# First chunk of a two-layer mixer kernel: eight one-block passes instead of five, with the rounding moved between engines

## The chip, the core and the metric

The kernel runs on one core of a Trainium2 chip. The metric is the device time of one execution in microseconds (us), the median of several runs. Times in the profile are us unless marked ns.

## What is computed

The program is a two-layer diffusion block over 1024 latent tokens and 256 context tokens, 1024 features wide. What matters here is the very beginning of layer 0, the modulated input and the first quarter of its input projection:

```
sh, sc, gt = split(silu(c) @ w_mod + b_mod, 3)     # c: a row of 1024, w_mod: 1024 x 3072
h  = x * (1 + sc) + sh                             # x: 1024 tokens x 1024
csh, csc, cgt = split(silu(c_ctx) @ w_mod + b_mod, 3)
hc = ctx * (1 + csc) + csh                         # ctx: 256 tokens x 1024
a, ga, u, v, gb = split([h; hc] @ w_in, ...)       # a: pooling branch, ga: its gate, ...
```

All else (pooling, spatial gating, Fourier mixing, latent attention, the output projections, the norms) comes after and is not touched.

## The kernel before

A float32 product is made of three passes of TensorE on rounded operands: an operand is split into a high part (rounded to the type fp32r) and a low part (the rest, rounded as well), and high x high, high x low and low x high are added up in PSUM. `split` (L103 to L107) makes both parts: a copy by VectorE (DVE) or ScalarE (ACT) gives the high part, a subtraction by GpSimd (POOL) or VectorE the low part.

The features lie on partitions, in eight row blocks of 128 (KT is 8, P is 128). The 1280 tokens (T) lie in the free dimension, in three segments, `SEG`: 512, 512 and 256 (context). The first chunk, 256 columns of the weight `ab_w_in` (called a1), is summed over the row blocks into five PSUM tiles `acc` (two column halves of each of the two long segments, and one tile for the short one), so that work can begin as soon as the first row block of `w_mod`, `w_in` and of the transposed input is there. `PASS` (L273) cuts the eight row blocks into passes of 1, 2, 2, 2 and 1. Per pass there are:

- `load` (L314): on the SyncE queue, the columns of `w_mod` for shift and scale of these row blocks (tiles `wm`), the rows of a1 (`raw_a`), and the rows of the transposed input (S, in the code `xT`).
- `mods` (L331): 16 float32 products of SiLU(c), SiLU(c_ctx) with `wm` (tile `md`), copied by DVE to `mrow` (L339). Each shows as two records in a trace.
- `mods_turn` (L341): transposes of `mrow` on TensorE (tile `pj`), then on DVE a sum (L347), two additions of the bias (L351) and 1 + scale (L352). The outcome is the tile `mod`: one column of shift and one of scale per row block.
- `split` of the a1 rows, and `fill` (L297) for each of five blocks of 256 tokens: one ACT operation per row block makes x * scale + shift in place (L303), then DVE makes the high part, and DVE (even blocks) or POOL (odd blocks) the low part; both cover two row blocks at once in a pass of two.
- `products` (L354) for each of the five `acc` tiles: three per row block (L363), twice that for the short segment.

`pin` keeps operations in the order of the program on their engine, so the loop sets what stands behind what: `mods` of the next pass stands on TensorE behind `acc` tile 0 of this one, and `mods_turn` behind tile 1 (tiles 2 and 3 in the first pass). Loads run one pass ahead: `load(p + 1)` is issued ahead of pass p. The tag wm has three buffers of 256 columns. Behind the last pass, `ga1`, the next 256 columns of `ab_w_in`, are split (ACT the high part, DVE the low one), and its products (`ps_mm`, L210) begin when the last `acc` product is through.

The whole of this takes the first 60 us of the program. The rest of the order is set by a planner, and by pattern strings for the attention.

Of the kernel before, what the change touches and what calls it, by code (L numbers as in the profile page):

```python
# [9 lines left out]
F32 = mybir.dt.float32  # L10
F32R = mybir.dt.float32r
AF = mybir.ActivationFunctionType
# [5 lines left out]
P = 128  # L18
# [3 lines left out]
T = S + C  # L22
NT = T // P
NL = S // P
KT = D // P
# [14 lines left out]
def _f(ap):  # L40
    return ap.bitcast(F32)


def hybrid_block(tc, A):
    nc = tc.nc
    ctx = ExitStack()
    with ctx:
        _body(nc, tc, A, ctx)


def _body(nc, tc, A, ctx):
    def pool(name, bufs=1, side=None, space=None, stack=ctx):
        kw = {}
        if side:
            kw["side"] = side
        if space is not None:
            kw["space"] = space
        return stack.enter_context(tc.tile_pool(name=name, bufs=bufs, reuse_waits="tile", **kw))
# [37 lines left out]
    def slot(pl, k, shape, dt, name):  # L96
        return pl.tile(shape, dt, tag=f"s{k}", name=name)


    def pin(ins):  # L100
        return tc.keep_in_program_order(ins)

    def split(dH, dL, src, h="v", l="p", ordered=False):  # L103

        keep = pin if ordered else (lambda ins: ins)
        keep(nc.vector.tensor_copy(dH, src) if h == "v" else nc.scalar.copy(dH, src))  # L106
        keep((nc.gpsimd if l == "p" else nc.vector).tensor_sub(dL, src, _f(dH)))  # L107
# [65 lines left out]
    def w_cols(w, c0, n):  # L173
        return w[:, c0:c0 + n].rearrange("(k p) n -> p k n", p=P)
# [65 lines left out]
    ld = pool("ld", stack=st0)  # L240
# [9 lines left out]
    mod0 = hp.tile([P, 16, 2], F32, name="mod0")  # L250
    mod1 = hp.tile([P, 16, 2], F32, name="mod1")
    S567 = [slot(keep if sl == 6 else var, sl, [P, 4096], F32, f"S{sl}") for sl in (5, 6, 7)]

    def ps_0(name, shape=(P, 512), tag="md"):
        return psums[-1].tile(list(shape), F32, tag=tag, name=name, bufs=1)
# [14 lines left out]


    SEG = ((0, 512), (512, 512), (1024, 256))
    PASS = ((0, 1), (1, 3), (3, 5), (5, 7), (7, 8))  # L273
    NP = len(PASS)
    st1 = ExitStack()
    w_a1 = w_cols(A["ab_w_in"], 256, 256)
    a1 = [wp.tile([P, 2048], F32R, tag=f"w{c_}", name=f"w{c_}_a1").rearrange("p (k n) -> p k n", k=KT) for c_ in "HL"]
# [3 lines left out]
    K0 = {k: (0, i) for i, k in enumerate((0, 1, 2, 7))} | {k: (1, k - 3) for k in range(3, 7)}  # L281
    K1 = {k: (k // 4, k % 4) for k in range(KT)}
    h0 = [[slot(keep if b in (0, 1) else var, b, [P, 2, 4, 512], F32R, f"h0_{b}") for b in (2 * sg, 2 * sg + 1)] for sg in range(2)]
    h0 += [slot(var, 4, [P, 2, KT, 256], F32R, "h0_4")]

    def tok(hs, at_, hl, k, a0, n):

        if a0 >= S:
            return hs[2][:, hl, k, a0 - S:a0 - S + n]
        half, i = at_[k]  # L290
        return hs[a0 // 512][half][:, hl, i, a0 % 512:a0 % 512 + n]


    at = ((0, 0), (0, 1), (0, 2), (1, 0), (1, 1), (2, 0), (2, 1), (1, 2))
    xT = [S567[i][:, j * T:(j + 1) * T] for i, j in at]

    def fill(p, b):  # L297

        k0, k1 = PASS[p]
        cnd = 0 if b < 4 else 1  # L300
        ts = slice(b * 256, (b + 1) * 256)
        for k in range(k0, k1):
            pin(nc.scalar.activation(xT[k][:, ts], xT[k][:, ts], AF.Identity,  # L303
                                     bias=mod0[:, k, cnd:cnd + 1], scale=mod0[:, 8 + k, cnd:cnd + 1]))
        i, j = at[k0]
        src = S567[i][:, j * T:(j + k1 - k0) * T].rearrange("p (k t) -> p k t", t=T)[:, :, ts]
        if b < 4:
            half, i = K0[k0]
            d = h0[b // 2][half][:, :, i:i + k1 - k0, b % 2 * 256:b % 2 * 256 + 256]
        else:  # L310
            d = h0[2][:, :, k0:k1, :]
        split(d[:, 0], d[:, 1], src, "v", "p" if b % 2 else "v", True)

    def load(p):  # L314
        k0, k1 = PASS[p]
        w = (k1 - k0) * P
        c = slice(k0 * P, k1 * P)
        wm = []
        for a in range(2):
            wm.append(ld.tile([P, KT, 256], F32, tag="wm", name=f"wm{p}{a}", bufs=3)[:, :, 0:w])  # L320
            src = w_cols(A["ab_w_mod"], a * D + k0 * P, w)
            n = KT if p else KT // 2
            for k in range(0, KT, n):
                nc.sync.dma_start(out=wm[a][:, k:k + n, :], in_=src[:, k:k + n, :])
        raw = wp.tile([P, 1024], F32, tag="raw", name=f"raw_a1_{p}", bufs=3)[:, 0:2 * w].rearrange("p (k n) -> p k n", n=256)
        nc.sync.dma_start(out=raw, in_=w_a1[:, k0:k1, :])
        for k in range(k0, k1):
            nc.sync.dma_start(out=xT[k], in_=A["xT"][k * P:(k + 1) * P, :])
        return wm, raw

    def mods(p, wm):  # L331
        md = ps_0(f"md{p}")
        w = (PASS[p][1] - PASS[p][0]) * P
        for a in range(2):
            for k in range(KT):
                g = k % 4
                pin(nc.tensor.matmul(md[32 * g:32 * g + 32, a * w:(a + 1) * w], lhsT=scp[:, k, :],
                                     rhs=wm[a][:, k, :], start=(k < 4), stop=(k >= 4)))
        pin(nc.vector.tensor_copy(mrow[:, :2 * w], md[:, :2 * w]))  # L339

    def mods_turn(p):  # L341
        pj = ps_0(f"pj{p}", (P, 4, 4, 32))
        k0, k1 = PASS[p]
        n = 2 * (k1 - k0)
        for j in range(n):
            pin(nc.tensor.transpose(pj[:, j].rearrange("p g c -> p (g c)"), mrow[:, j * P:(j + 1) * P], ident))
        pin(nc.vector.tensor_reduce(out=msum[:, :n], in_=pj[:, :n, :, 0:2].rearrange("p j g c -> p j c g"), axis=AX.X, op=ALU.add))  # L347
        m = mod0.rearrange("p (a k) c -> p a k c", a=2)[:, :, k0:k1, :]
        bm = cols[:, R_BM0:R_BM0 + 16].rearrange("p (a k) -> p a k", a=2)[:, :, k0:k1]
        for c2 in range(2):  # L350
            pin(nc.vector.tensor_add(m[:, :, :, c2], msum[:, :n, c2].rearrange("p (a k) -> p a k", a=2), bm))  # L351
        pin(nc.vector.tensor_scalar(m[:, 1], m[:, 1], 1.0, 1.0, op0=ALU.mult, op1=ALU.add))  # L352

    def products(p, u):  # L354
        sg, j_ = UNITS[u]
        a0, nt = SEG[sg]
        js = (0, 1) if j_ is None else (j_,)
        for j in js:
            c = slice(j * P, (j + 1) * P)
            o = acc[u][:, j * nt:(j + 1) * nt] if j_ is None else acc[u]  # L360
            for k in range(*PASS[p]):
                for n, (w, x) in enumerate(((0, 0), (0, 1), (1, 0))):
                    pin(nc.tensor.matmul(o, lhsT=a1[w][:, k, c], rhs=tok(h0, K0, x, k, a0, nt),  # L363
                                         start=(k + n == 0 and j == js[0]), stop=(k == KT - 1 and n == 2 and j == js[-1])))

    W.add("ga1", w_cols(A["ab_w_in"], 768, 256), KT, 256, eng=("s", "v"))
    raws = {}
    wm, raws[0] = load(0)
    mods(0, wm)
    mods_turn(0)  # L370
    for p in range(NP):
        if p < NP - 1:
            wm, raws[p + 1] = load(p + 1)
        k0, k1 = PASS[p]
        split(a1[0][:, k0:k1, :], a1[1][:, k0:k1, :], raws[p], "v", "p", True)
        if p == NP - 2:
            W.fetch("ga1", 1e9)
        for b in range(5):
            fill(p, b)
        if p == NP - 1:  # L380
            for i in range(2):
                W.step("ga1", i)
        for b in range(5):
            products(p, b)
            if p < NP - 1 and b == (0 if p else 2):
                mods(p + 1, wm)
            if p < NP - 1 and b == (1 if p else 3):
                mods_turn(p + 1)
    st0.close()

# [230 lines left out]
    for ch in (1, 0):  # L621
# [11 lines left out]
        if ch == 1:  # L633
            for u, (sg, j_) in enumerate(UNITS):
                o, n = OFF[sg], SEG[sg][1]
# [171 lines left out]
    for t in range(NT):  # L807
        src = A["x"][t * P:(t + 1) * P, :] if t < NL else A["ctx"][(t - NL) * P:(t - NL + 1) * P, :]
# [758 lines left out]
```

## Time and profile before

| | |
|---|---|
| median of 3 runs | 1137.46 us (1137.27 to 1138.54) |
| the profiled execution, its own time | 1138.53 us |
| its span, first to last instruction | 1136.7 us |
| PE busy | 1077.7 us, 95% of the span |
| PE weight loads busy | 917.5 us, 81% |
| DVE busy | 827.1 us, 73% |
| ACT busy | 456.3 us, 40% |
| POOL busy | 524.2 us, 46% |
| mean granted TensorE clock | 0.977 of full speed |
| last product of the first chunk issued, first of ga1 begins | 60.38 us |

PE is TensorE's matmuls, PEld its weight loads, SPq SyncE's DMA queue. Busy shares are means over stages that have different limits. Matmuls are pipelined: rows of PE overlap, and the distance from one start to the next says more than a duration. "[0.74 <-POOL h L107]" behind a row means that the engine was idle for 0.74 us and what ended that.

### The profile page before, as it was taken

What the parts mean: (1) busy time and instruction counts of PE and PEld (TensorE: products, weight loads), DVE (VectorE), ACT (ScalarE), POOL (GpSimd) and SP (SyncE); (2) the same over time, 40 slices, a digit from 0 to 9 for tenths busy, and PEclk for the clock granted to TensorE, in tenths of its full rate; (3) what the DMA queues carried; (4) which work ended last, traced back from release to release, by engine and by line L of the source; (5) the groups of instructions that cost most, each with busy time, mean ns of one, the idle gap of its engine ahead of it and who ended that gap; (6) DMA issues with size and microseconds to landing.
All of it is one profiled execution on the core that took longest, in us unless ns stands there. A gap on an engine that the chain in (4) does not pass through costs nothing.

```text
span 1136.7 us, 16517 instructions
## 1 busy us (share of the span) xinstructions
PE 1077.7 (95%) x5986; PEld 917.5 (81%) x5986; DVE 827.1 (73%) x1713; ACT 456.3 (40%) x1096; POOL 524.2 (46%) x449
## 2 busy tenths in 40 slices
PE   6999999899999999999999999999999999999884
PEld 4788887778878888897888877889899898887664
DVE  4683547899987767767200175988999989977998
ACT  3421222221211233531021244887888888860000
POOL 2362321555563433112481234855556556657442
PEclk7999999989999999999999999999999999999897
DMA  9630110235543322404311110000000010214221
GB/s 345 222 95 29 47 56 1 60 108 168 166 156 122 104 101 71 148 1 154 106 56 37 34 53 22 1 1 2 1 1 1 1 57 1 75 38 143 85 77 67
DMA packets 46993, 85.58 MB, mean 75 GB/s; under 512 B 2928, under 2 KB 27632, under 8 KB 46912
## 3 DMA queue, kind: packets, MB, share of 16 engines
q1 hardware_dynamic: 44096, 76.60, 21.2%
q0 software_dynamic: 1664, 5.84, 1.4%
q10 hardware_dynamic: 1152, 2.10, 0.5%
q8 instruction: 47, 0.77, 0.3%
q14 instruction: 34, 0.28, 0.1%
HBM read 76.13 MB, written 8.39 MB: 74 GB/s over the span
## 4 chain that ended last, share of the span: by engine, by line
PE 65%; DVE 23%; issue 4%; POOL 3%; ACT 3%; DMA 1%; SPq 0%; DVEq 0%; POOLq 0%; ACTq 0%
PE ps_mm L210 19%; PE ps_o L442 10%; PE s L1096 8%; PE ps_n L442 6%; PE av L1314 5%; PE pt_p L1289 5%; PE acc L363 2%; PE ps_y L1049 2%; DVE acc L499 2%; DVE mx L1255 2%; DVE rz L1477 2%; PE ps_c L210 2%; DVE rz L1446 1%; PE pq L1106 1%; DVE rs_tz L227 1%
## 5 line engine op out<-in xcount | busy, mean ns | idle before, releaser
L1096 PE MATMUL s<-kT,qT 96*128 96x512 f32 (+1 forms) x576 | 147.8, 370 | 3.7 <-ACT p L1267 2.7
L1267 ACT ACTIVATE p<-s,mx 128x512 f32<-128x512 f32 (+1 forms) x192 | 118.7, 624 | 17.1 <-DVE mx L1278 16.1
L1255 DVE TENSOR_REDUCE mx<-s 128x1 f32<-128x512 f32 (+1 forms) x192 | 112.1, 594 | 8.9 <-PE s L1096 7.0
L1298 DVE TENSOR_TENSOR pT<-pt_p,pT 128x512 fp32r<-128x512 f32 x160 | 108.1, 684 | 10.1 <-ACT pT L1294 8.1
L1275 POOL TENSOR_SCALAR p<-p,mx 128x1280 f32<-128x1280 f32 x64 | 85.6, 1341 | 42.1 <-ACT pT L1294 11.9
L1096 PEld LDWEIGHTS s<-kT,qT 96*128 96x128 f32 x576 | 90.7, 189 | 16.3 <-ACT p L1267 6.3
L1294 ACT CAST pT<-pt_p 128x512 fp32r<-128x512 f32 x160 | 92.8, 587 | 19.6 <-PE pt_p L1289 12.3
L1289 PE MATMUL pt_p<-ident,p 128*128 128x128 f32 x640 | 92.9, 273 | 0.9 <-DVE kT L1202 0.5
L1314 PE MATMUL av<-pT,V 128*128 128x256 f32 x480 | 78.9, 291 | 2.1 <-DVE pT L1298 2.1
L1289 PEld LDWEIGHTS pt_p<-ident,p 128*128 128x128 f32 x640 | 74.4, 140 | 7.4 <-ACT q L1112 1.1
L1314 PEld LDWEIGHTS av<-pT,V 128*128 128x128 f32 x480 | 67.5, 189 | 6.8 <-DVE pT L1298 2.5
L442 PE MATMUL ps_o<-wo,yhl 128*128 128x512 f32 x240 | 57.2, 391 | 0.0
L442 PE MATMUL ps_o<-wH_o,yhl 128*128 128x512 f32 x160 | 53.8, 397 | 0.0
L210 PE MATMUL ps_mm<-h,wH_u 128*128 128x512 f32 (+1 forms) x192 | 53.4, 367 | 0.0
L442 PE MATMUL ps_n<-wH_v,h 128*128 128x512 f32 x160 | 52.1, 395 | 0.0
L442 PEld LDWEIGHTS ps_o<-wo,yhl 128*128 128x128 f32 x240 | 44.8, 188 | 9.1
L442 PE MATMUL ps_z<-wz,yz 128*128 128x512 f32 (+1 forms) x216 | 47.3, 376 | 4.8 <-POOL wz L107 2.4
L210 PE MATMUL ps_mm<-h,wH_gb 128*128 128x512 f32 (+1 forms) x192 | 51.7, 357 | 0.0
L210 PE MATMUL ps_mm<-h,wH_ga 128*128 128x512 f32 (+1 forms) x192 | 51.2, 354 | 0.0
L442 PEld LDWEIGHTS ps_z<-wz,yz 128*128 128x128 f32 x216 | 38.2, 193 | 13.0 <-POOL wz L107 2.9
L442 PE MATMUL ps_z<-wH_z,yz 128*128 128x512 f32 (+1 forms) x112 | 36.8, 408 | 8.2 <-DVE yz L106 7.4
L210 PE MATMUL ps_c<-wH_c,h 128*128 128x416 f32 (+1 forms) x160 | 42.3, 341 | 0.0
(390 smaller groups left out, 2876.2 us busy)
## 6 DMA issues: line engine op xcount, KB each, us to landing
rawmm<-in_cd_w_mod SPq DMA_DIRECT2D x16, 512.0 KB, 3.6
wm<-in_ab_w_mod SPq DMA_DIRECT2D x6, 1024.0 KB, 8.2
S<-in_xT SPq DMA_DIRECT2D x8, 640.0 KB, 7.6
rawmg<-in_ab_w_mod SPq DMA_DIRECT2D x8, 512.0 KB, 3.6
raw_o<-in_ab_w_out SPq DMA_DIRECT2D x8, 512.0 KB, 3.8
xr<-in_x SPq DMA_DIRECT2D x8, 512.0 KB, 3.5
xn_d<-S POOLq DMA_DIRECT2D x8, 512.0 KB, 3.0
rawmg<-in_cd_w_mod SPq DMA_DIRECT2D x8, 512.0 KB, 4.3
```

The lines of the kernel that those rows point to most:

```text
L210: nc.tensor.matmul(out, lhsT=a, rhs=b, start=(i == 0), stop=(i == n - 1))
L363: pin(nc.tensor.matmul(o, lhsT=a1[w][:, k, c], rhs=tok(h0, K0, x, k, a0, nt), start=(k + n == 0 and j == js[0]), stop=(k == KT - 1 and n = ...
L442: nc.tensor.matmul(ps, lhsT=lhsT(a, kk), rhs=w[b][:, k, :], start=(kk + i == 0), stop=(kk == KT - 1 and i == 2))
L499: pin(nc.vector.scalar_tensor_tensor(o, raw[:, c], s, o, op0=ALU.mult, op1=ALU.add))
L1096: pin(nc.tensor.matmul(out, lhsT=a, rhs=b, start=(i == 0), stop=(i == 2)))
L1255: pin(nc.vector.tensor_reduce(out=mx[:, j:j + 1], in_=ps, axis=AX.X, op=ALU.max))
L1267: pin(nc.scalar.activation(p32[:, e0:e0 + en], sc[e], AF.Exp, bias=mx[:, 3:4], scale=1.0, accum_out=mx[:, 4 + e:5 + e]))
L1275: pin(nc.gpsimd.tensor_scalar(p32, p32, mx[:, 8:9], 1.0, op0=ALU.mult, op1=ALU.mult))
L1289: pin(nc.tensor.transpose(pt[:, kk * 256 + i * P:kk * 256 + (i + 1) * P], P_of[2 * B + i][:, k * P:(k + 1) * P], ident))
L1294: pin(nc.scalar.copy(pT_of[B, kp][:, 0, :], pt))
L1298: pin(nc.vector.tensor_sub(pT[:, 1, :], pt, _f(pT[:, 0, :])))
L1314: pin(nc.tensor.matmul(av, lhsT=vv, rhs=pT[:, hl, kk * 256:(kk + 1) * 256], start=(k == 0 and hl == 0), stop=(k == NT - 1 and hl == 1)))
```

## The change

`PASS` becomes eight passes of one row block. `fill` goes by the three token segments instead of five blocks of 256: ACT writes the high part itself, straight from the input (first operation), then makes x * scale + shift in place (second one), and DVE subtracts. GpSimd has no part in the chunk any more; the low parts of the a1 rows go to DVE too. `load` fills `wm` tiles of 128 columns, six of them, and runs three passes ahead. `mods` of the next pass stands behind `acc` tile 1, `mods_turn` behind tile 2. The lines behind L309 move up by six.

```
 
 
     SEG = ((0, 512), (512, 512), (1024, 256))
-    PASS = ((0, 1), (1, 3), (3, 5), (5, 7), (7, 8))
+    PASS = tuple((k, k + 1) for k in range(KT))
     NP = len(PASS)
     st1 = ExitStack()
     w_a1 = w_cols(A["ab_w_in"], 256, 256)
@@ -294,22 +294,16 @@
     at = ((0, 0), (0, 1), (0, 2), (1, 0), (1, 1), (2, 0), (2, 1), (1, 2))
     xT = [S567[i][:, j * T:(j + 1) * T] for i, j in at]
 
-    def fill(p, b):
-
-        k0, k1 = PASS[p]
-        cnd = 0 if b < 4 else 1
-        ts = slice(b * 256, (b + 1) * 256)
-        for k in range(k0, k1):
-            pin(nc.scalar.activation(xT[k][:, ts], xT[k][:, ts], AF.Identity,
-                                     bias=mod0[:, k, cnd:cnd + 1], scale=mod0[:, 8 + k, cnd:cnd + 1]))
-        i, j = at[k0]
-        src = S567[i][:, j * T:(j + k1 - k0) * T].rearrange("p (k t) -> p k t", t=T)[:, :, ts]
-        if b < 4:
-            half, i = K0[k0]
-            d = h0[b // 2][half][:, :, i:i + k1 - k0, b % 2 * 256:b % 2 * 256 + 256]
-        else:
-            d = h0[2][:, :, k0:k1, :]
-        split(d[:, 0], d[:, 1], src, "v", "p" if b % 2 else "v", True)
+    def fill(p, sg):
+
+        cnd = 0 if sg < 2 else 1
+        a0, n = SEG[sg]
+        x = xT[p][:, a0:a0 + n]
+        hi, lo = (tok(h0, K0, a, p, a0, n) for a in (0, 1))
+        bias, scale = mod0[:, p, cnd:cnd + 1], mod0[:, 8 + p, cnd:cnd + 1]
+        pin(nc.scalar.activation(hi, x, AF.Identity, bias=bias, scale=scale))
+        pin(nc.scalar.activation(x, x, AF.Identity, bias=bias, scale=scale))
+        pin(nc.vector.tensor_sub(lo, x, _f(hi)))
 
     def load(p):
         k0, k1 = PASS[p]
@@ -317,7 +311,7 @@
         c = slice(k0 * P, k1 * P)
         wm = []
         for a in range(2):
-            wm.append(ld.tile([P, KT, 256], F32, tag="wm", name=f"wm{p}{a}", bufs=3)[:, :, 0:w])
+            wm.append(ld.tile([P, KT, 128], F32, tag="wm", name=f"wm{p}{a}", bufs=6))
             src = w_cols(A["ab_w_mod"], a * D + k0 * P, w)
             n = KT if p else KT // 2
             for k in range(0, KT, n):
@@ -364,27 +358,27 @@
                                          start=(k + n == 0 and j == js[0]), stop=(k == KT - 1 and n == 2 and j == js[-1])))
 
     W.add("ga1", w_cols(A["ab_w_in"], 768, 256), KT, 256, eng=("s", "v"))
-    raws = {}
-    wm, raws[0] = load(0)
-    mods(0, wm)
+    wms, raws = {}, {}
+    for p in range(3):
+        wms[p], raws[p] = load(p)
+    mods(0, wms[0])
     mods_turn(0)
     for p in range(NP):
-        if p < NP - 1:
-            wm, raws[p + 1] = load(p + 1)
-        k0, k1 = PASS[p]
-        split(a1[0][:, k0:k1, :], a1[1][:, k0:k1, :], raws[p], "v", "p", True)
+        split(a1[0][:, p:p + 1, :], a1[1][:, p:p + 1, :], raws[p], "v", "v", True)
+        if p + 3 < NP:
+            wms[p + 3], raws[p + 3] = load(p + 3)
         if p == NP - 2:
             W.fetch("ga1", 1e9)
-        for b in range(5):
-            fill(p, b)
+        for sg in range(3):
+            fill(p, sg)
         if p == NP - 1:
             for i in range(2):
                 W.step("ga1", i)
-        for b in range(5):
-            products(p, b)
-            if p < NP - 1 and b == (0 if p else 2):
-                mods(p + 1, wm)
-            if p < NP - 1 and b == (1 if p else 3):
+        for u in range(5):
+            products(p, u)
+            if p < NP - 1 and u == 1:
+                mods(p + 1, wms[p + 1])
+            if p < NP - 1 and u == 2:
                 mods_turn(p + 1)
     st0.close()
 
```

On TensorE, for the pass that takes row block 4 after the change, and the two row blocks 3 and 4 before (h is the split input, wH_a and wL_a the two parts of a1, md and pj the tiles of `mods` and `mods_turn` for the pass to come). Before:

```order
L363 MATMUL acc_100<-h_1_121,wH_a_118 128x512 x2
L363 MATMUL acc_100<-h_1_121,wL_a_119 128x512
L363 MATMUL acc_100<-h_1_121,wH_a_118 128x512 x2
L363 MATMUL acc_100<-h_1_121,wL_a_119 128x512
L337 MATMUL md_358<-wm_322,scp 32x256 x8
L337 MATMUL md_358<-wm_324,scp 32x256 x8
L363 MATMUL acc_101<-h_1_121,wH_a_118 128x512 x2
L363 MATMUL acc_101<-h_1_121,wL_a_119 128x512
L363 MATMUL acc_101<-h_1_121,wH_a_118 128x512 x2
L363 MATMUL acc_101<-h_1_121,wL_a_119 128x512
L346 MATMUL pj_382<-ident,mrow 128x128 x4
```

After:

```order
L357 MATMUL acc_100<-h_1_121,wH_a_118 128x512 x2
L357 MATMUL acc_100<-h_1_121,wL_a_119 128x512
L357 MATMUL acc_101<-h_1_121,wH_a_118 128x512 x2
L357 MATMUL acc_101<-h_1_121,wL_a_119 128x512
L331 MATMUL md_441<-wm_297,scp 32x128 x8
L331 MATMUL md_441<-wm_299,scp 32x128 x8
L357 MATMUL acc_102<-h_3_123,wH_a_118 128x512 x2
L357 MATMUL acc_102<-h_3_123,wL_a_119 128x512
L340 MATMUL pj_462<-ident,mrow 128x128 x2
```

The products of the next pass's shift and scale stand behind six products of this pass in both, but now once per row block; three products instead of six stand between them and their transposes.

On DVE, one pass. Before (two row blocks):

```order
L106 CAST wH_a_118<-raw_a_2_233 128x512
L106 CAST h_1_121<-S_94 128x2x256
L107 TENSOR_TENSOR h_1_121<-S_94,h_1_121 128x2x256
L106 CAST h_1_121<-S_94 128x2x256
L106 CAST h_3_123<-S_94 128x2x256
L107 TENSOR_TENSOR h_3_123<-S_94,h_3_123 128x2x256
L106 CAST h_3_123<-S_94 128x2x256
L106 CAST h_4_124<-S_94 128x512
L107 TENSOR_TENSOR h_4_124<-S_94,h_4_124 128x512
L339 COPY mrow<-md_358 128x512
```

After (one row block):

```order
L106 CAST wH_a_118<-raw_a_4_240 128x256
L107 TENSOR_TENSOR wL_a_119<-raw_a_4_240,wH_a_118 128x256
L306 TENSOR_TENSOR h_1_121<-S_94,h_1_121 128x512
L306 TENSOR_TENSOR h_3_123<-S_94,h_3_123 128x512
L306 TENSOR_TENSOR h_4_124<-S_94,h_4_124 128x256
L333 COPY mrow<-md_441 128x256
```

The five casts of the input are gone from DVE, and the three subtractions of the segments stand ahead of the copy of the next pass's shift and scale.

On ACT, at the end of the last pass, after the change (pad takes the finished `acc` tile 0):

```order
L304 ACTIVATE h_2_122<-S_94,mod_91 128x512
L305 ACTIVATE S_94<-S_94,mod_91 128x512
L304 ACTIVATE h_4_124<-S_94,mod_91 128x256
L631 COPY pad_637<-acc_100 128x512
L305 ACTIVATE S_94<-S_94,mod_91 128x256
L106 CAST wH_ga_534<-raw_ga_0_536 128x1024
L106 CAST wH_ga_534<-raw_ga_4_538 128x1024
```

The evacuation of `acc` tile 0 has moved ahead of the last part of the fill; before, all evacuations stood behind the casts for ga1.

## Rows read from the trace of the kernel before

**Rows 1.** Stretches between finished `mod` tiles: PE, PEld, DVE, ACT, POOL, clock, DMA, GB/s

```profile
10.04:20.76 10.72, 8.83 (x54) 5.37 (x54) 4.92 (x15) 2.57 (x5) 2.19 (x3) 0.68 1.07 396
20.76:33.73 12.97, 9.35 (x53) 5.53 (x53) 7.99 (x15) 5.02 (x10) 3.92 (x3) 0.74 0.94 339
33.73:44.19 10.46, 9.72 (x73) 7.16 (x73) 8.03 (x15) 5.03 (x10) 3.95 (x3) 1.00 0.79 273
44.19:53.58 9.39, 8.64 (x71) 6.82 (x71) 7.66 (x16) 5.04 (x10) 4.82 (x5) 1.00 0.58 192
```

**Rows 2.** Groups by shape, 0 to 62 us: count, busy us, mean ns, idle before

```profile
L303 ACT ACTIVATE S<-S,mod 128x256 f32<-128x256 f32 x40 | 20.2, 588 | 33.1 <-DVE mod L352 33.1
...
L637 ACT COPY S<-acc 128x512 f32<-128x512 f32 x2 | 1.2, 588 | 0.1
...
L637 ACT COPY S<-acc 128x256 f32<-128x256 f32 x1 | 0.4, 378 | 0.0
...
L106 DVE CAST wH_a<-raw_a 128x512 fp32r<-128x512 f32 x3 | 1.3, 421 | 0.0
```

**Rows 3.** Timeline of the third pass, 33 to 45 us

```profile
33.76 5.03 ACT L303 ACTIVATE S<-S,mod 128x256 f32<-128x256 f32 x10 [7.95 <-DVE mod L352]
...
35.74 0.69 DVE L107 TENSOR_TENSOR h<-S,h 128x512 fp32r<-128x512 f32 x1
...
38.18 0.50 PE L363 MATMUL acc<-h,wH_a 128*128 128x512 f32 x1 [0.74 <-POOL h L107]
...
39.53 1.93 PE L337 MATMUL md<-wm,scp 128*32 128x256 f32 x32
```

**Rows 4.** Timeline of the fourth pass, whose `mods` are for one row block

```profile
50.00 1.08 PE L337 MATMUL md<-wm,scp 128*32 128x128 f32 x32
...
51.01 0.73 PE L363 MATMUL acc<-h,wH_a 128*128 128x512 f32 x2
...
52.52 0.38 PE L346 MATMUL pj<-ident,mrow 128*128 128x128 f32 x2
...
52.93 0.17 DVE L347 TENSOR_REDUCE msum<-pj 128x4 f32<-128x16 f32 x1 [0.64 <-PE pj L346]
```

**Rows 5.** Timeline of the first pass, TensorE at half clock

```profile
13.74 1.05 PE L363 MATMUL acc<-h,wH_a 128*128 128x512 f32 x2
...
14.59 0.63 PE L363 MATMUL acc<-h,wL_a 128*128 128x512 f32 x1
```

**Rows 6.** Stretches elsewhere in which PE has gaps

```profile
668.90:672.20 3.30, 2.10 (x10) 1.47 (x10) 3.30 (x10) 1.62 (x3) 1.48 (x5) 1.00 0.00 0
672.20:675.70 3.50, 3.50 (x12) 2.82 (x11) 3.50 (x15) 3.05 (x5) 2.41 (x2) 0.51 0.02 5
1115.10:1122.00 6.90, 4.58 (x39) 4.54 (x39) 6.55 (x14) 0.20 (x1) 0.00 (x0) 1.00 0.21 76
```

**Rows 7.** Timeline of the end of the chunk

```profile
56.10 1.98 ACT L106 CAST wH_ga<-raw_ga 128x1024 fp32r<-128x1024 f32 x2
...
57.86 2.35 DVE L107 TENSOR_TENSOR wL_ga<-raw_ga,wH_ga 128x1024 fp32r<-128x1024 f32 x2
...
60.38 0.63 PE L210 MATMUL ps_mm<-h,wH_ga 128*128 128x512 f32 x2
```

**Rows 8.** Stretches, DMA at its fullest with short and with longer rows

```profile
4.00:6.00 2.00, 1.94 (x13) 1.65 (x15) 0.00 (x0) 0.00 (x0) 0.00 (x0) 1.00 0.95 267
...
34.00:36.00 2.00, 2.00 (x12) 1.70 (x11) 1.13 (x3) 2.00 (x5) 1.29 (x1) 1.00 1.10 425
```

**Rows 9.** Timeline of 218 to 230 us, a later stage

```profile
220.24 2.39 POOL L107 TENSOR_TENSOR wL_u<-raw_u,wH_u 128x1024 fp32r<-128x1024 f32 x1 [3.69 <-DVE wH_u L106]
...
220.35 2.83 DVE L106 CAST wH_u<-raw_u 128x1024 fp32r<-128x1024 f32 x1
...
228.74 0.58 PE L691 MATMUL pf<-ws,vH 128*128 128x256 f32 x1 [4.42 <-ACT vH L106]
```

**Rows 10.** Stretch around that wait

```profile
228.00:236.00 8.00, 6.78 (x17) 5.02 (x17) 6.75 (x25) 2.96 (x7) 1.90 (x3) 0.57 0.07 29
```

## The prediction

> **What bounds the kernel now.** I read the page's slices first: TensorE is busy nearly everywhere, so time is won or lost where it waits or runs at a low clock, and the first 60 us have both. The stretches between one finished `mod` tile and the next [rows 1] show four turns, for 1, 2, 2 and 2 row blocks: 10.72, 12.97, 10.46 and 9.39 us. In the first two the granted clock is 0.68 and 0.74, partly at the lower of its two levels (1.2 against 2.4 GHz), in the last two 1.00. DMA is full in the first turn and falls to 0.58 of its time in the fourth, so transfers don't set these turns. The groups by shape name what does [rows 2]: ACT stood still for 33.1 us ahead of its fill operations, all of it for `mod`. `mod` comes from `mods`, which stand on TensorE behind products that need the fill, which needs the last `mod`. That is a loop through ACT, DVE, TensorE and DVE again, and its length per row block is the time of the chunk. In the third turn [rows 3] one sees it: `mod` done at 33.73, fill from 33.76, the low part ready for the product at 38.18, `md` at 39.53, next `mod` at 44.19. It is 10.46 us for two blocks, 5.2 per block.
>
> **The loop after the change.** There are eight passes, so seven turns of the loop instead of four, one row block each. Worked out at full clock from the moment at which `mod` is ready:
>
> - ACT, segment 0: it starts 0.03 after `mod` (33.73 to 33.76). A fill operation of 256 columns takes 0.588 and ten of them take 5.03, so one starts 0.50 after the other [rows 2, 3]. The form with 512 columns isn't in the trace. From below it costs what the 512-column evacuation does, 0.588; from above two of the 256-column form, 1.18. I take 256 columns more at the price by which the evacuations differ, 588 - 378 = 210 ns [rows 2]: 0.80 for one, 0.71 apart. The high part is there at 0.83, the shifted input at 0.03 + 0.71 + 0.80 = 1.54.
> - DVE: 0.04 to hand over (an estimate), then the low part, 0.69 as in the row of the same shape that ran with POOL out of its way [rows 3]: 2.27. That POOL is gone is why I don't take more.
> - TensorE: the second product of tile 0 needs that low part, so it and four more products (one of tile 0, three of tile 1) lie on the path. In the third pass also five products lie between the wait and `md`: 38.18 to 39.53, 1.35 [rows 3]. With 0.06 to hand over: 3.68.
> - `mods` for one block: 1.01 from their start to the next product [rows 4]. Then three products of tile 2 stand ahead of `pj`; in the fourth pass it is six, 1.51 us from 51.01 to 52.52, or 0.25 each; three leave 0.76. `pj` starts at 5.45. The copy to `mrow` has to fit beside those three products instead of six; by the same rows it just does, and should it stick out, a tenth or two per turn is lost.
> - `pj` to the sum, 52.52 to 52.93: 0.41 [rows 4]; the sum and the rest to the finished `mod` at 53.58 [rows 1]: 0.65. Together 6.51 us a turn; with the bounds for ACT (0.2 less per operation, or 0.35 more, two of them in series) 6.1 to 7.2.
>
> So a turn of one block costs 6.51, where one of two blocks cost 10.46: per block 1.3 us more. The edit takes DVE's casts and all of POOL's work away, but in a loop of latencies what counts is what stands in series, and a fixed part (handing over, five products, `mods`, `pj`, sum) is now paid seven times instead of four.
>
> The first turn runs at half clock. Products there start 0.85 / 2 = 0.43 apart instead of 0.25 [rows 5]: 5 x 0.18 = 0.9 more, `mods` at half clock 1.0 more, the products of tile 2 between nothing and 0.5, depending on when the clock rises. I take 6.51 + 2.2 = 8.7 (bounds 8.4 and 8.9). The second turn of before, at 0.74 of the clock, is the one that should gain: I let the clock stay at 1.00 from the second turn on. TensorE's gaps in a turn are by this sum about 0.4 us (tiles 3 and 4 end at 7.1, the next high part is there at 6.51 + 0.9) and 1.2 (from the first product to the low part), and elsewhere a stretch with 2.3 us without work (6.90 less 4.58) kept its clock [rows 6]. That it falls is rival 1.
>
> **The last pass and what follows.** `mod` for the eighth block: 10.04 + 8.7 + 6 x 6.51 = 57.8, where before the last one came at 53.58. Of the last fill, ACT makes four operations of 512 and one of 256, then the evacuation of tile 0 that now stands there, then one of 256: 0.03 + 4 x 0.71 + 0.50 + 0.58 + 0.59 = 4.5. The low part of 256 columns on DVE (about 0.42, an estimate from 0.69 at 512) and five products of half the width, 0.13 each, follow: TensorE is free for ga1 at 57.8 + 5.7 = 63.5. The casts of ga1's weights on ACT start at 4.5 as well and take 1.98 for two, the low parts on DVE 2.35 for two [rows 7]. The first low part is ready at 4.5 + 1.0 + 1.2 = 6.7, while ga1's third product wants it at 5.7 + 0.5: with the handing over a stall of 0.6. Before, both low parts were ready at 60.21 and the first product began at 60.38, with no stall. The sum: 63.5 + 0.6 - 60.4 = **3.7 us later**. From there the order of the engines is nearly the same as before, so I let the rest shift by that, though each change of phase between DVE and POOL can give or take a microsecond or two.
>
> **Loads and the split of the a1 rows**: nothing in the sum. A pass brings 1.05 MB of `wm`, 0.66 of input and 0.13 of a1 rows. With rows of 512 bytes, which all `wm` transfers now have, full engines moved 267 GB/s; with longer rows 425 [rows 8]. That is 3.9 + 1.9 = 5.8 us a pass, less than the turn of 6.51 and begun three passes ahead. If that cover went, a pass would wait for its `wm`. The page "DMA: Bandwidth & Descriptors" of the Trainium skill (section Specifications) says that 512 bytes are enough for the full rate; by that a pass would load in 4.3 us and could never be late. The trace doesn't agree (267 against 425), so a late load stays among the rivals. DVE's two operations on the a1 rows end before the first low part is due, since DVE only waits for ACT there.
>
> **Against which time.** The profiled execution took 1138.53 us, of which its span is 1136.7. It lies 1.07 above the median of three runs, 1137.46. The sum gives 1142.2 against the former, and against the median **1141.2 us**, which I predict.
>
> **Rivals.**
>
> 1. *The clock falls back in the passes* (slower still). A turn leaves TensorE without work twice: from the end of the short tile to the first product of the next pass (0.4), then until the low part (1.2). Rows elsewhere point both ways: after a stretch with 2.10 us of work in 3.30 the clock was at 0.51, and across a single gap (4.58 in 6.90) it stayed at 1.00 [rows 6]; in the third turn 0.74 did no harm [rows 1, 3]. A turn at half clock costs what the first one did, 2.2 more. One to three such turns: 2.2 to 6.6 more, with two 1145.6. Chance 0.2.
> 2. *A later collision goes away* (faster). A cast of 1024 columns, 0.84 by the row of 512, took 2.83 beside a POOL subtraction, and TensorE then stood 4.42 us [rows 2, 9]; over the 8 us behind it the clock was 0.57 [rows 10], which on 6.78 us of work costs 6.78 x 0.43 = 2.9. Another phase between POOL and DVE may avoid it: 4.4 + 2.9 = 7.3 less, 1141.2 - 7.3 = 1133.9. It decides if POOL's subtraction starts a microsecond off DVE's cast. For it speaks that POOL has no work in the chunk any more; against it that the order is the same and the products pace both. Chance 0.08.
> 3. *The loads are late.* If short rows went at 200 GB/s, a pass would need 5.2 + 1.9 = 7.1 and the last four turns 0.6 more each: 1143.6. Chance 0.06.
> 4. *The delay is taken up later* or the first turns run better than I think: within 0.2%. Chance 0.1.
>
> **How the numbers follow.** My own case has 0.56, with 1138.5 to 1145.5 by its bounds (six turns of 6.1 to 7.2, the first of 8.4 to 8.9). 0.2% is 2.3 us, about what a measurement can tell from no change. Slower is the sum of my case, rivals 1 and 3: 0.82; same 0.10; faster 0.08. The range takes in these bounds and two and a half turns of rival 1 at the top: 1138.2 to 1147.0.
>
> **What would show it.** Seven waits of ACT for `mod`, together still over 15 us; `mod` tiles some 6.5 us apart; between them gaps of TensorE before the second product of tile 0 that end with DVE's low part; the clock at 1.00 from about 17 us on; POOL idle; ga1 from about 64. Wrong it is if turns are below 6 us (then the loop isn't what I say), if TensorE waits for `wm`, or if the ga1 stage starts late and the end doesn't.

## The result and the profile after

The change makes the kernel slower: 1144.77 us (median of 4 runs, 1143.92 to 1145.17) against 1137.38 (1137.27 to 1138.54) for the kernel before, a ratio of 1.0058 with a 95% interval of 1.0045 to 1.0070. Run again later with more rounds (e11_change_again below), it was 1145.76, ratio 1.0072, 1.0060 to 1.0085. The forecast, 1141.2, had the sign and the cause right; it is 3.6 us short, half of the difference (the range went to 1147.0). The profiled execution took 1145.17 with a span of 1143.3; before it was 1138.53 and 1136.7. So the pair of profiles differs by 6.6 us, and TensorE is already 5.5 late when the products of `ga1` are on their way.

The stretches from one first fill of ACT to the next, which answer to [rows 1] (columns as there: PE, PEld, DVE, ACT, POOL, clock, DMA share, GB/s; the last row ends with the first product of `ga1`):

```profile
10.60:19.06 8.46, 6.82 (x48) 4.76 (x49) 3.43 (x11) 4.23 (x6) 0.00 (x0) 0.63 1.07 356
19.06:25.77 6.71, 5.45 (x54) 3.93 (x54) 3.44 (x11) 4.24 (x6) 0.00 (x0) 1.00 0.98 302
...
32.50:39.22 6.72, 5.46 (x54) 3.93 (x54) 3.43 (x11) 4.24 (x6) 0.00 (x0) 1.00 1.04 315
...
52.66:59.37 6.71, 5.46 (x54) 3.93 (x54) 3.44 (x11) 4.24 (x6) 1.06 (x5) 1.00 0.27 82
59.37:65.33 5.96, 4.69 (x24) 3.46 (x24) 2.70 (x6) 5.89 (x9) 0.00 (x0) 1.00 0.22 52
```

Seven turns instead of four; the six at full clock take 6.71 to 6.73 us each, whatever DMA does (share 0.98 in one, 0.27 in another). No engine is full: PE is busy 5.46 of 6.72, ACT 4.24, DVE 3.43. That is how a loop of latencies looks. The clock is at 1.00 from 17.16 us to the end of the chunk.

One turn in the timeline, third column on: engine, line, operation, tiles, shape, and in brackets the idle time before it with what ended that:

```profile
32.50 0.82 ACT L304 ACTIVATE h<-S,mod 128x512 fp32r<-128x512 f32 x1 [2.38 <-DVE mod L346]
33.35 0.81 ACT L305 ACTIVATE S<-S,mod 128x512 f32<-128x512 f32 x1
...
34.20 0.69 DVE L306 TENSOR_TENSOR h<-S,h 128x512 fp32r<-128x512 f32 x1 [1.08 <-ACT S L305]
...
36.87 0.42 DVE L306 TENSOR_TENSOR h<-S,h 128x256 fp32r<-128x256 f32 x1 [0.43 <-ACT S L305]
37.45 0.42 DVE L333 COPY mrow<-md 128x256 f32<-128x256 f32 x1 [0.15 <-PE md L331]
38.53 0.17 DVE L341 TENSOR_REDUCE msum<-pj 128x4 f32<-128x16 f32 x1 [0.66 <-PE pj L340]
...
39.22 0.82 ACT L304 ACTIVATE h<-S,mod 128x512 fp32r<-128x512 f32 x1 [2.38 <-DVE mod L346]
```

The loop is the one that the prediction drew. Note DVE: its last low part begins at 36.87, and the copy to `mrow` right behind it, after only 0.15 us of waiting. That nearness decides two experiments below.

The waits of the same stretch (10 to 66 us; total us, times, longest) say the same: ACT waits for `mod` eight times (seven of them, without the first of 7.8, make 18.4 us), TensorE for DVE's low part eight times, POOL once, for nearly all of the chunk. The one wait for a load in this view is POOL's, 0.6 us for the weights of `ga1`; none stands in the loop.

```profile
POOL S L622 <- DVE h L306: 55.1, 1, 55.1
ACT h L304 <- DVE mod L346: 26.2, 8, 7.8
DVE h L306 <- ACT S L305: 19.3, 24, 1.1
...
PE acc L357 <- DVE h L306: 8.3, 8, 1.1
```

The end of the chunk, which answers to [rows 7]:

```profile
63.96 1.98 ACT L106 CAST wH_ga<-raw_ga 128x1024 fp32r<-128x1024 f32 x2
...
65.03 2.36 DVE L107 TENSOR_TENSOR wL_ga<-raw_ga,wH_ga 128x1024 fp32r<-128x1024 f32 x2 [0.51 <-ACT wH_ga L106]
...
65.33 0.63 PE L210 MATMUL ps_mm<-h,wH_ga 128*128 128x512 f32 x2
66.31 0.50 PE L210 MATMUL ps_mm<-h,wL_ga 128*128 128x512 f32 x1 [0.34 <-DVE wL_ga L107]
```

The first product of `ga1` starts at 65.33 instead of 60.38. Two products 0.23 apart should let the third start at 65.79; it waits for its low part until 66.31, a stall of 0.5.

Behind that the shift is rigid for a long way: matched product by product, TensorE is 5.55 to 5.6 us late at 61, 100, 150 and 180 us of the kernel before. One such pair, first from the kernel before, then from the changed one:

```profile
150.78 0.28 PE L210 MATMUL ps_p<-dH,pwH 128*128 128x256 f32 x1
```

```profile
156.33 0.28 PE L210 MATMUL ps_p<-dH,pwH 128*128 128x256 f32 x1
```

Later it moves in jumps between 4.2 and 7.5; the large ones, at 673, 1095, 1109 and 1120 us of the kernel before, lie where one of the two has a low-clock stretch (the granted clock at 0.50) and the other has not. The place of the collision in [rows 9] looks as before:

```profile
225.80 2.40 POOL L107 TENSOR_TENSOR wL_u<-raw_u,wH_u 128x1024 fp32r<-128x1024 f32 x1 [3.69 <-DVE wH_u L106]
...
225.91 2.84 DVE L106 CAST wH_u<-raw_u 128x1024 fp32r<-128x1024 f32 x1
...
234.32 0.39 PE L685 MATMUL pf<-ws,vH 128*128 128x256 f32 x1 [4.14 <-ACT vH L106]
```

The last jump lies in the last products of the kernel. The rows of the kernel before, of the changed one, of the run e11_change_again (the changed kernel unedited) and of the run e4_loads_one_ahead (below; its order behind `ga1` is the changed kernel's), all from the timeline of TensorE:

```profile
1117.46 5.92 PE L442 MATMUL ps_z<-wz,yz 128*128 128x256 f32 x48 [2.33 <-DVE rz L1445]
```

```profile
1123.33 7.23 PE L436 MATMUL ps_z<-wz,yz 128*128 128x256 f32 x48 [3.88 <-DVE rz L1439]
```

```profile
1123.96 7.41 PE L436 MATMUL ps_z<-wz,yz 128*128 128x256 f32 x48 [2.79 <-DVE rz L1439]
```

```profile
1125.94 5.92 PE L436 MATMUL ps_z<-wz,yz 128*128 128x256 f32 x48 [2.29 <-DVE rz L1439]
```

The same 48 products take 5.92 us where the granted clock is 1.00 throughout, and 7.23 where it is 0.80 on the average (1123.33 to 1130.56 in the changed kernel). So they can add more than 1 us, but they need not: in e4 they are as short as before, and the span of its profile, the slowest of its four executions, is 9.3 us longer than that of the kernel before.

### The profile page after: what moved, and what is told of

Read it like the earlier page. It is cut to its first block, busy times and chain, and to the rows that moved or that the text cites. A ratio compares the mean times of both kernels' runs of the same rounds, so it can differ in the third digit from the quotient of the medians.

```text
span 1143.3 us, 16735 instructions
## 1 busy us (share of the span) xinstructions
PE 1077.9 (94%) x6082; PEld 916.5 (80%) x6082; DVE 815.1 (71%) x1723; ACT 469.6 (41%) x1104; POOL 510.4 (45%) x434
## 4 chain that ended last, share of the span: by engine, by line
PE 63%; DVE 23%; issue 4%; ACT 4%; POOL 3%; DMA 3%; SPq 0%; DVEq 0%; ACTq 0%; POOLq 0%
PE ps_mm L210 18%; PE ps_o L436 8%; PE s L1090 8%; PE ps_n L436 6%; PE av L1308 5%; PE pt_p L1283 4%; PE ps_y L1043 2%; DVE rz L1471 2%; DVE mx L1249 2%; PE ps_c L210 2%; PE acc L357 2%; DVE rz L1440 2%; PE pq L1100 1%; DVE acc L493 1%; DVE rs_tz L227 1%
## 5 line engine op out<-in xcount | busy, mean ns | idle before, releaser
L436 PE MATMUL ps_z<-wH_z,yz 128*128 128x512 f32 (+1 forms) x112 | 34.5, 387 | 9.1 <-DVE yz L106 7.2
```

Of the source, the lines that this page charges most:

```text
L436: nc.tensor.matmul(ps, lhsT=lhsT(a, kk), rhs=w[b][:, k, :], start=(kk + i == 0), stop=(kk == KT - 1 and i == 2))
```

## The experiments

All times are medians, with the kernel before timed beside them on the same chip (1138.24 for the first four runs, 1138.13 for the next four, 1137.70 for the last two).

**The two halves of the change apart.** Run e1_new_fill_old_passes leaves `PASS`, loads and `mods` as before and takes only the new fill, per segment and row block:

```
-    def fill(p, b):
...
+        for k in range(*PASS[p]):
+            pin(nc.scalar.activation(hi, x, AF.Identity, bias=bias, scale=scale))
+            pin(nc.scalar.activation(x, x, AF.Identity, bias=bias, scale=scale))
+            pin(nc.vector.tensor_sub(lo, x, _f(hi)))
```

> The kernel before with its five passes, its loads and its place for the mods products; only the fill is the changed one (ScalarE writes the high part and then the shifted input, VectorE subtracts, three segments, GpSimd has nothing in the chunk). My theory is that the number of turns of the loop is what costs, and not who rounds: the low part of the second row block is ready some 3.8 us after mod, against 4.4 in the third turn of before, but the copy to mrow stands on VectorE behind the last low part, which ScalarE's twelve operations (8 x 0.71 + 4 x 0.50 = 7.7 us) set, so a turn of two blocks takes about 9.8 us against 10.46, the last pass 6.2 against 6.8, and ga1's first product begins some 2 us earlier than before: 1133 to 1138 us, likeliest 1135.4. Rival: two passes over the input on ScalarE are what costs; then turns of two blocks take 11 us or more and the time is 1139 or more.

Measured: 1140.81, 2.6 us more than before (ratio 1.0022, 1.0007 to 1.0038). My number was missed, in the rival's direction: the two turns of two blocks at full clock take 11.10 and 10.59 us, not 9.8, against 10.46 and 9.39 in [rows 1], and `ga1` starts at 63.04, 2.7 late. DVE and TensorE in the first of the two:

```profile
41.63 0.42 DVE L307 TENSOR_TENSOR h<-S,h 128x256 fp32r<-128x256 f32 x1 [0.70 <-ACT S L306]
41.97 0.68 DVE L334 COPY mrow<-md 128x512 f32<-128x512 f32 x1
...
42.71 0.66 PE L341 MATMUL pj<-ident,mrow 128*128 128x128 f32 x4 [1.39 <-DVE mrow L334]
43.40 0.19 DVE L342 TENSOR_REDUCE msum<-pj 128x8 f32<-128x32 f32 x1 [0.75 <-PE pj L341]
```

I had named the mechanism, `mrow` standing on DVE behind the last low part, and had ACT's twelve operations too short: 33.01 to 41.59 is 8.6 us, since the second operation on a segment starts 0.84 after the first, where the next segment's follows 0.72 later (0.78 on the average, not 0.71), and the short ones start 0.5 to 0.6 apart. TensorE then stands 1.39 us for `mrow`.

Run e2_old_fill_new_passes is the other half: the changed kernel with the fill of before.

```
-        for sg in range(3):
-            fill(p, sg)
+        for b in range(5):
+            fill(p, b)
```

> The changed kernel with its eight passes, its loads and its place for the mods products; only the fill is that of before (five blocks of 256 tokens, VectorE rounds, VectorE or GpSimd subtracts). If the number of turns is what costs, the turns stay between 6.5 and 7.6 us (the second block's low part, by GpSimd, is ready no earlier than the changed kernel's 1.7 + 0.69), ga1 begins at 64 to 71 us and the time is 1144 to 1150, likeliest 1147. Rival: the fill on ScalarE is what costs; then turns fall to 6 us or less and the time to about 1139.

Measured: 1145.49, 7.3 more than before (ratio 1.0057, 1.0040 to 1.0074); turns of 6.91 to 6.92, `ga1` from 66.91.

```profile
33.10:40.03 6.93, 5.47 (x54) 3.94 (x54) 4.64 (x15) 2.57 (x6) 2.20 (x3) 1.00 1.05 344
```

So the passes, with the new places of loads and `mods`, cost all of it without the new fill. The new fill, which harms the old passes by 2.6, is slightly better than the old one within the new passes (6.72 a turn against 6.92). Those 0.2 us are the net of two parts that e8 below takes apart.

**Take the loop away.** Run e3_mods_two_ahead makes shift and scale one pass earlier:

```
-            if p < NP - 1 and u == 1:
-                mods(p + 1, wms[p + 1])
-            if p < NP - 1 and u == 2:
-                mods_turn(p + 1)
+            for q, ua, ub in ([(1, 0, 1), (2, 2, 3)] if p == 0 else [(p + 2, 1, 2)]):
+                if q < NP and u == ua:
+                    mods(q, wms[q])
+                if q < NP and u == ub:
+                    mods_turn(q)
```

> The changed kernel, with the products and the transposes that make shift and scale (mods, mods_turn) one pass further ahead: pass 0 makes those of blocks 1 and 2, pass p those of block p + 2, at the same places. If the loop through mods is what paces the passes, ScalarE waits for mod no more after the first pass; a pass then takes what TensorE has to do (12 products 0.25 apart, 6 at half width, mods 1.08, two transposes: about 5.0 us) or what its loads take (5.7 us from one load of the input to the next in the changed kernel). With the loads as the bound the last input lands at about 50 us, ga1 begins at about 56 instead of 65.3, and the time is about 1135.5 (1132 to 1139). Rival: the fill itself, three dependent operations on ScalarE and VectorE ahead of five products, paces a pass whatever mods do; then turns stay above 6.3 us and the time within 2.5 us of the changed kernel's.

Measured: 1137.05, just below the kernel before (ratio 0.9989, 0.9980 to 0.9999), some 8 us less than the changed kernel. The passes are 5.55 to 5.73 us apart and `ga1` starts at 57.04, one us later than I said. What is left shows on TensorE, at the second product of a pass:

```profile
33.25 0.50 PE L357 MATMUL acc<-h,wH_a 128*128 128x512 f32 x1 [0.36 <-DVE h L306]
...
57.04 0.63 PE L210 MATMUL ps_mm<-h,wH_ga 128*128 128x512 f32 x2
```

DVE works in order: 1 + scale of block p + 2, then the two operations on the a1 rows of the next pass, then its first low part, for which TensorE waits. Run e5_two_ahead_a1_early therefore moves the a1 rows up by a pass as well (`halve` is the line taken out, made a function; `halve(0)` stands ahead of the loop):

```
-        split(a1[0][:, p:p + 1, :], a1[1][:, p:p + 1, :], raws[p], "v", "v", True)
...
         for sg in range(3):
             fill(p, sg)
+        halve(p + 1)
```

> The kernel with mods two passes ahead, and VectorE's two operations on the a1 rows of a pass (0.28 and 0.43 us) moved from the head of that pass into the pass before it. In the run with mods two ahead TensorE still stood 0.36 us a pass for the first low part, which is VectorE's next operation but two after 1 + scale. If that order on VectorE is what is left, the 0.36 goes, six or seven passes shrink from 5.6 to about 5.25 us, unless the loads hold them at 5.65, and ga1 begins 1 to 2.5 us earlier than at 57.0; the time is 1134.5 to 1136.5. Rival: the loads set the pass already, or the end of the kernel takes the gain back; then the time stays within 0.8 us of that run's, 1137.05.

Measured: 1134.73, ratio 0.9974 (0.9963 to 0.9985): faster than both kernels, by 3.4 us than the one before and by some 10 than the change. `ga1` starts at 55.32. Three of its turns:

```profile
25.57:30.49 4.92, 4.92 (x55) 3.88 (x54) 3.17 (x10) 4.82 (x8) 0.00 (x0) 1.00 1.07 340
30.49:36.75 6.26, 5.18 (x55) 3.85 (x54) 3.17 (x10) 5.27 (x8) 0.00 (x0) 1.00 1.03 315
...
42.07:46.99 4.92, 4.92 (x55) 3.88 (x54) 3.18 (x10) 3.94 (x6) 0.17 (x3) 1.00 1.08 327
```

In the first and the last of these TensorE is busy 4.92 of 4.92: there it is the bound at last. In the turn of 6.26 a load is late:

```profile
35.15 0.65 PE L331 MATMUL md<-wm,scp 128*32 128x128 f32 x16 [0.99 <-DMA wm<-in_ab_w_mod]
```

So the rival with late loads, wrong for the change, comes true as soon as a pass is shorter than its loads. Longer rows, the `wm` of two blocks in one transfer, were not tried.

**How far ahead the loads run.** Run e4_loads_one_ahead issues them one pass ahead and gives `wm` four buffers instead of six.

```
-            wm.append(ld.tile([P, KT, 128], F32, tag="wm", name=f"wm{p}{a}", bufs=6))
+            wm.append(ld.tile([P, KT, 128], F32, tag="wm", name=f"wm{p}{a}", bufs=4))
...
-        if p + 3 < NP:
-            wms[p + 3], raws[p + 3] = load(p + 3)
+        if p + 1 < NP:
+            wms[p + 1], raws[p + 1] = load(p + 1)
```

> The changed kernel with loads issued one pass ahead instead of three, and room for the wm tiles of two passes instead of three. By my theory nothing waits for a load: turns stay at 6.7 us and the time within 1.2 us of the changed kernel's. Rival: the depth carries the passes; then TensorE waits for wm in some of them, and the time is 2 to 8 us more.

Measured: 1145.68 (ratio 1.0063, 1.0047 to 1.0079), with turns of 6.70 to 6.75 at full clock: the deeper loads do nothing for this change, and no product waits for a load (waits of 10 to 67 us). In e3 and e5 a pass uses the `wm` of the block two ahead, so these need them at least two passes ahead; which depth they need wasn't tried.

**What else the turn consists of.** Run e6_mods_one_unit_earlier puts `mods` behind tile 0 and `mods_turn` behind tile 1 (`u == 0`, `u == 1` instead of 1 and 2).

> The changed kernel with mods behind tile 0 (as before the change) instead of tile 1, and mods_turn behind tile 1: three products less ahead of mods. If the chain through the five products alone sets the turn, each shrinks by three products, 0.7 us, to 6.0 and the time by 7 x 0.7 = 4.9 to about 1140. Rival, which I now hold for likelier: ScalarE's six operations and VectorE's last low part end 4.8 us after the turn begins, the copy to mrow stands right behind that on VectorE and began at 4.95, so only 0.15 us a turn is to be had, turns stay at 6.55 and the time at about 1143.8.

Measured: 1142.12 (ratio 1.0033, 1.0021 to 1.0045), turns of 6.35. Three products less on the path are worth 0.7 us; 0.37 came. Where the rest went:

```profile
35.07 0.43 DVE L306 TENSOR_TENSOR h<-S,h 128x256 fp32r<-128x256 f32 x1 [0.43 <-ACT S L305]
35.41 0.42 DVE L333 COPY mrow<-md 128x256 f32<-128x256 f32 x1
...
36.36 0.17 DVE L341 TENSOR_REDUCE msum<-pj 128x4 f32<-128x16 f32 x1 [0.53 <-PE pj L340]
```

The copy to `mrow` follows the last low part without a gap. The rival's bound holds, but it is looser than I put it, since `pj` no longer waits for the products ahead of it: it starts 0.06 after the end of the copy (35.89), where in the changed kernel it was 0.24 (38.11). So two chains of nearly equal length closed the turn: fill to products to `mods`, and fill to last low part to `mrow`.

Run e8_vector_rounds gives the rounding back to VectorE, in the new passes:

```
-        pin(nc.scalar.activation(hi, x, AF.Identity, bias=bias, scale=scale))
         pin(nc.scalar.activation(x, x, AF.Identity, bias=bias, scale=scale))
+        pin(nc.vector.tensor_copy(hi, x))
```

> The changed kernel, with the high part rounded by VectorE from the shifted input (ScalarE makes one operation per segment instead of two, VectorE two instead of one); nothing else is changed. The low part of segment 0 is then ready after 0.03 + 0.82 + 0.05 + 0.42 + 0.69 = 2.0 us instead of 2.4, and VectorE's last low part 3.9 instead of 4.8 us after the turn begins. If the rounding on ScalarE lies on the loop, turns shrink by 0.3 to 0.4 to 6.35 us and the time to 1142.0 (1141 to 1143.5). Rival: VectorE's six operations now crowd mrow and the sums; then turns are 6.7 or longer and the time is no better than the changed kernel's.

Measured: 1141.22, 3.1 more than before (ratio 1.0026, 1.0017 to 1.0036), turns of 6.32 to 6.34, as expected. ScalarE's second operation in series costs 0.4 us a turn and, against the 7.4 of the change, about half of what the change costs:

```profile
31.67:38.01 6.34, 5.46 (x54) 3.93 (x54) 4.40 (x14) 2.02 (x4) 0.00 (x0) 1.00 1.03 313
...
32.52 0.43 DVE L305 CAST h<-S 128x512 fp32r<-128x512 f32 x1 [0.23 <-ACT S L304]
32.98 0.69 DVE L306 TENSOR_TENSOR h<-S,h 128x512 fp32r<-128x512 f32 x1
...
33.73 0.50 PE L357 MATMUL acc<-h,wH_a 128*128 128x512 f32 x1 [0.23 <-DVE h L306]
```

Cast and subtraction end 2.0 us after ACT's start at 31.67, where ACT's two operations and the subtraction took 2.4. Beside e2, whose turns take 6.92 with VectorE rounding as well, this kernel lacks only the five blocks of 256 tokens and GpSimd's part: the other half of the new fill, three segments and all low parts on VectorE, is worth 0.6 us a turn, and rounding on ScalarE takes 0.4 of that back. How the 0.6 is shared between the segments and GpSimd isn't shown.

Run e6 leaves 4.0 us of the loss and e8 3.1. Both edits together were not tried, so what eight passes cost at their best with `mods` one pass ahead is open.

In run e9_both_ahead_vector_rounds the same edit is made to the kernel of e5.

> The kernel of the run e5_two_ahead_a1_early (mods two passes ahead, a1 rows one pass ahead), with VectorE rounding as in e8_vector_rounds. In e5 four of the passes came 4.9 to 5.3 us apart, which is what TensorE has to do in one, and the fill is made a pass ahead. If TensorE is the bound there, who rounds no longer matters: within 0.8 us of 1134.7. Rival: ScalarE's 4.3 us a pass still hold something (the last pass, whose input lands late); then the time falls by 1 us or more. A third way: VectorE gets too full (1.8 + 1.14 + 0.7 + 1.2 of 4.9 us) and the time rises by 1 us or more.

Measured: 1135.76 (ratio 0.9983, 0.9974 to 0.9992), with turns of 5.36 instead of 4.92 and `ga1` from 57.37 instead of 55.32. That is the third way by the turns; in time the intervals of e5 and e9 overlap. With the loop gone, DVE is the engine that must not be loaded.

```profile
43.92:49.28 5.36, 5.21 (x53) 3.85 (x52) 4.32 (x14) 2.01 (x3) 0.17 (x3) 1.00 1.08 364
```

ACT falls from between 3.94 and 5.27 us a turn to 2.01, DVE rises from 3.18 to 4.32, in order with what TensorE waits for (DVE's low part, six times between 18 and 57 us). What is right for the rounding depends on which chain closes the pass.

**Is a delay handed on one for one?** Run e7_before_and_5us is the kernel before with 23 more products ahead of `ga1`:

```
+    again = ps_0("again")
+    for n in range(23):
+        pin(nc.tensor.matmul(again, lhsT=a1[0][:, 0, 0:P], rhs=tok(h0, K0, 0, 0, 0, 512), start=True, stop=True))
     st0.close()
```

> The kernel before with 23 products of 512 columns more on TensorE, 0.23 us each by the distance of its neighbours, between the last acc product and ga1 (they write a tile that nobody reads): 5.3 us of delay at full clock, and nothing else changed. If what follows ga1 shifts rigidly, the time is before + 5.3, about 1143.5. Rival: a delay at this place costs more than itself, since the later stages fall into other phases (in the pair of profiles ga1's products were 5.7 late and the end 6.6); then the time is before + 6.5 or more. If later waits take it up, before + 4 or less.

Measured: 1142.62, 4.5 us more (ratio 1.0037, 1.0023 to 1.0051, which is 2.6 to 5.8 us). The inserted products took 62.20 to 67.44, 5.24 us. A delay of this size is passed on, and not enlarged (the 6.5 of the rival lies outside the interval; that 1 us is taken up later does not):

```profile
62.20 5.40 PE L391 MATMUL again<-h,wH_a 128*128 128x512 f32 x23
67.44 0.62 PE L210 MATMUL ps_mm<-h,wH_ga 128*128 128x512 f32 x2
```

In this profile TensorE is 7.0 late behind the inserted products, since the first fill came 1.0 later (11.05 against 10.07) and the first turns were longer; the span is 6.5 longer.

**The change once more.** Run e11_change_again is the changed kernel, unedited.

> The changed kernel once more, unedited, with more rounds, for the size of the whole difference. By the run with 23 products more, a delay ahead of ga1 is handed on one for one, so the changed kernel's 5.7 us at ga1 should be most of it: before + 5.7 to + 7, 1143.8 to 1145.1. Rival: what follows ga1 adds 1.5 us or more of its own each time; then before + 7.2 or more, 1145.3 or more.

Measured: 1145.76, 8.1 us more than before (6.8 to 9.7 by its interval), which is the rival's side. Its profile doesn't bear the rival's reason out. `ga1` began at 66.55, 6.2 late: the first fill came at 11.05, 1.0 later than in the profile of before and 0.45 later than in the first profile of the change, and the first turn took 9.22 us instead of 8.46. From 62 to 180 us the products are 6.8 late, and the span is 7.2 longer than before. So nearly all of the difference was lost ahead of `ga1`.

## Why the prediction was right, and by how much not

- *The bound* was right: the loop through fill, low part, products, `mods` and `mod` set the passes. Shown by e3, where only its links move and some 8 us go, and by e5.
- *The cost of a turn*, 6.51, measured 6.72. By its terms, from one fill to the next: to the second product 2.30 forecast, 2.44 measured (32.50 to 34.94); five products 1.35 and 1.36; `mods` 1.01 and 1.01; three products 0.76 and 0.80; `pj` to the sum 0.41 and 0.42; the rest to the next fill 0.68 and 0.69. No term was missing; the one mis-sized is ACT's distance, 0.85 between the first operation and the second where I took 0.71. Handing over from ACT to DVE and from DVE to TensorE, estimates of 0.04 and 0.06, took 0.04 and 0.05 (34.16 to 34.20, 34.89 to 34.94). Six turns: 1.3 us.
- *The operation of 512 columns on ACT*, an estimate of 0.80 between 0.588 and 1.18, is 0.80 to 0.82.
- *The first turn at half clock*: 8.7 forecast, 8.46 measured. *From the last fill to `ga1`*: 5.7 and 5.96. *The stall behind it*: 0.6 and 0.5.
- *The start*: I took the first `mod` from the profile of before. It came 0.5 us later, and nothing says that this is an effect of the change: in twelve profiles the first fill starts between 9.88 and 11.09, at 10.07 and 11.05 for the same unedited beginning (before and e7).
- Together 0.5 - 0.2 + 1.3 + 0.3 - 0.1 = 1.8 more than the 3.7 of the sum: 5.5, which is what the third product of `ga1` shows (60.84 before, 0.46 behind the first one in [rows 7], and 66.31).
- *"From there the rest shifts by that"*, plus or minus a microsecond or two: true to a few hundredths up to 180 us. From there to the end the shift went from 5.5 to 6.6 in the pair of profiles, from 6.8 to 7.2 in e11, from 6.6 to 9.3 in e4 and from 7.0 to 6.5 in e7, against the same profile of before. So the end gives or takes some us, as I had said, and e7 speaks against an enlargement as such. The last products, 5.92 us before and in e4, 7.23 in the changed kernel and 7.4 in the profiles of e1, e3, e5, e7, e9 and e11, are one place where it happens. Why a low-clock stretch hits them in some and not in others isn't settled.
- *The number.* The medians lie 7.4 and 8.1 apart, the sum had 3.7. The turns add 1.3, and that is shown. The rest was a start and a first turn, which differ by up to 1 us and 0.8 us between two profiles of kernels that are the same up to there, and the low-clock stretches behind `ga1`. How much each of these holds of the medians isn't shown, since each run has one profile. The range held the result with room to spare because it was wide, 8.8 us for a difference of 7.4.
- *Rival 1, the clock falls back in the passes*: no, in none of the nine profiles of eight passes once it had risen. The slack in a turn (5.46 busy of 6.72) did it no harm, while the old passes fall to half clock a second time in the kernel before, at 23.7 us.
- *Rival 2, a later collision goes away*: no, see the rows at 225 us: cast 2.84, TensorE idle 4.14.
- *Rival 3, late loads*: no for the change (e4), yes behind it (e5). In the changed kernel the issues of the input rows lie 5.6 us apart on the average while DMA is full:

```profile
21.77 0.42 SPq L322 DMA_DIRECT2D S<-in_xT  x1
...
44.30 0.42 SPq L322 DMA_DIRECT2D S<-in_xT  x1
```

That is (44.30 - 21.77) / 4 for 1.84 MB, 327 GB/s, near the 5.8 of my sum by two rates; at the 425 GB/s of the longer rows [rows 8] it would have been 4.3, and the wait of 0.99 for `wm` in e5 fits the slower rate. By the page "DMA: Bandwidth & Descriptors" of the Trainium skill (section Specifications) rows of 512 bytes go at the full rate. The trace of this mix of rows doesn't agree (327 against 425), and the measurement decides.

What I missed in kind is DVE's order. I had asked whether the copy to `mrow` fits beside three products, but not that it stands behind the last low part, so a second chain was only 0.15 us shorter than the one I added up. It set the turn in e1, where I had by then named it, and it is why e6 gave half of what three products would have.

## What to carry to other kernels

Splitting work into more passes so that it starts earlier pays the fixed part of a loop once per pass. Look first whether the loop has to be closed within a pass: making what the next pass needs (shift and scale, then the parts of the a1 rows) one pass earlier turned eight passes from 7 us slower than five into 3 us faster, with the same instructions. And where two engines each work in order, follow both queues round the loop: the second longest chain limits what shortening the longest one gives.

## What the runs showed of the hardware

The first fill starts up to 1.2 us apart from one profile to the next (9.88 to 11.09 us; 1.0 between two kernels that are the same up to there), which is half of the 0.2% that I called measurable. Versions with the same order of products behind `ga1` can differ there by 1 us and more, by where the low-clock stretches fall: the 48 last products of 256 columns took 5.92 us (before, e4), 7.23 (the change), 7.4 (six runs), 8.20 (e2), 8.54 (e6) and 8.68 (e8). On ScalarE an operation of 512 columns that overwrites the input of the one just ahead started 0.83 to 0.85 us after it, one on another segment 0.72 (the change, e1).
